# Seven products over the whole contraction for all eight pairs of weight blocks, and one pool for the large scratch

## The chip, the cores and the metric

The kernel runs on one core of a Trainium2 chip. The metric is device time in microseconds (us) of one execution; the time of a kernel is the median of its runs. A run goes through these engines: TensorE (PE, with its weight load PEld), VectorE (DVE), ScalarE (ACT), GpSimd (POOL) and SyncE (SP), which here only issues DMAs. Each engine works through its own queue of instructions in order; semaphores make one engine wait for another.

## The reference, cut to what matters

One layer of a decoder trunk over 528 tokens (16 meta tokens and 512 of the sequence), width 2048: an RMS norm, one input projection, three token mixers side by side (gated DeltaNet with 6 heads, GLA with 5, forgetting attention with 5), a SiLU gate per head, and one output projection with a residual add and a final norm.

```python
h = rms_norm(x, norm_w)
proj = h @ w_in                      # 2048 x some 7600 columns, split into heads
...
o_fox = forgetting_attention(to_heads(fq) * FOX_D ** -0.5, to_heads(fk), to_heads(fv), log_f)
o_fox = o_fox.reshape(fz.shape) * jax.nn.silu(fz)
o = jnp.concatenate([o_dn, o_gla, o_fox], axis=-1)[:, PAD:]
return x + o @ w_out                 # then the final rms_norm
```

Each attention head needs four blocks of 128 columns of `w_in`: `fk`, `fq`, `fv` and `fz` (keys, queries, values, gate). All arithmetic is float32; a product is formed from two parts of each factor (`hi` and `lo`), as hi·hi + hi·lo + lo·hi, so three matmuls stand for one.

## The kernel before, in words

**Layout.** Activations are held transposed: 16 chunks of 128 contraction rows by 528 tokens, each as two tiles, `xh[k]` and `xl[k]`. A block of 128 weight columns is two halves of 128 x 1024 (`w_in[b, 0]` for chunks 0 to 7, `w_in[b, 1]` for chunks 8 to 15). `load_half` (L145) loads one half into `raw`, ACT writes `hi` (L166), DVE writes `lo` (L167). `raw`, `hi` and `lo` have two buffers each (pool `wp`).

**A plain block** (`inproj`, L237) multiplies both halves with all tokens. With the meta tokens it is 96 matmuls of 264 columns, without them 48 of 512 columns (L223).

**Order.** DeltaNet gates; two groups of three DeltaNet heads (`dn_keys`, `dn_values`, `dn_queries`, `dn_inverse`, `dn_mix`); the five GLA gates; three `gla_pair`s; five `fox_head`s; the output projection. The order of the instructions on every engine is written at build time by a list scheduler, which goes by program order as priority, by its own model of times and by which buffers are free; `split` is given priority over everything, and some small matmuls of GLA are tied behind a numbered matmul of a projection (`PLACE`, L191).

**Seven products.** For attention heads 1 to 4 two blocks `one` and `two` form a pair, (`fk`, `fq`) or (`fv`, `fz`). Cut tokens into two halves of 264 (`lo_`, `hi_`), the contraction into two halves (`up`: chunks 0 to 7, `dn`: 8 to 15) and the columns into `one` and `two`: the 2 x 2 by 2 x 2 block product needs eight products, or seven if sums of operands are used (Strassen and Winograd). The sums of activations are `t1`, `t2` and `t4`, made on POOL with their `hi` and `lo` parts on ACT and DVE (`x_sums`, L462), and a difference that overwrites `xh[k][:, HT:]` and `xl[k][:, HT:]` (`x_last`, L489: three DVE operations per chunk ahead, then one on ACT and one on DVE once no plain block needs the old values). The sums of weights, `ti`, are made in DRAM by DMAs of POOL's queue: four copies and four accumulating copies per pair (`in_jobs`, L441). The output projection has such sums of its own (`tw`, `out_jobs`). Both are "chores": every `load_half` issues `rate` steps of them, paced behind a `split`.

Here only four of the eight chunks of each half (`NK = 4`) go by the seven products; the other four (`r0`, `r1`) go by plain ones in the same function `inproj_pair` (L504), which loads its weights with `tile_of` (L512) in six tiles and splits them in pieces of 512 columns. A pair is 180 matmuls: 144 of 264 columns and 36 of 248. The first pair, (`fk`, `fq`) of head 1, is left out (`SKIP = 1`) and runs as two plain blocks (L1108 to L1110), so there are seven pairs. For the first of them the sums are used late (`LATE = 1`).

**Buffers.** `hp`: 32 tiles for `xh` and `xl`. `zp`: 12 tiles of 128 x 528 for the gates, and for `t1`, `t2`, `t4` of chunks 0 to 2. `six`: 8 large buffers (128 x 1584) for the operands of the mixers, the sums of chunk 3, and so on. `row`: 7 of 128 x 531. `t15`: 6 of 128 x 384. Gates of the first eight heads are written to DRAM (`zd`) and read back for the output projection (L1256); the other eight stay in `zp` and in the tiles of the attention heads.

Of the kernel before, what the change touches and what calls it, by code (L numbers as in the profile page):

```python
# [18 lines left out]
P = 128  # L19
D = 2048  # L20
KT = D // P
NM = 16
# [12 lines left out]
NK = 4  # L35
H1 = 1
SKIP = 1
LATE = 1
ZK = 3
# [44 lines left out]
def tile_hybrid_trunk(ctx, tc, xT, xtok, mtok, w_gate, w_in, w_out, w_dn, consts, lmask, fin_w, out, dbg=None):  # L84
# [7 lines left out]
    zp = pool("zp", 12)  # L92
    six = pool("six", 8)
# [34 lines left out]
    wgk = cst.tile([48, 320], F32R, name="wgk")  # L128
# [30 lines left out]
    def split(raw, hi, lo, neg=False):  # L159
        with tc.high_priority(offset=1000000):  # L160
            if neg:
                pace[0] = A.activation(hi, raw, AF.Copy, scale=-1.0).ins  # L162
                pace[1] = V.scalar_tensor_tensor(out=lo, in0=raw, scalar=-1.0, in1=hi.bitcast(F32), op0=ALU.mult,  # L163
                                                 op1=ALU.subtract).ins
            else:
                pace[0] = A.copy(hi, raw).ins  # L166
                pace[1] = V.tensor_tensor(out=lo, in0=raw, in1=hi.bitcast(F32), op=ALU.subtract).ins  # L167
# [9 lines left out]
    def load_rows(src, name):  # L177

        n = src.shape[-1]
        raw = row(f"raw{name}")[:, :n]  # L180
        nc.sync.dma_start(out=raw, in_=src)
        hi, lo = (zp.tile([P, 512], F32R, tag="zs", name=f"w{i}{name}")[:, :n] for i in ("hi", "lo"))
        split(raw, hi, lo)
        return hi, lo
# [171 lines left out]
    zs = {}  # L356

    def gate_z(kind, h, t=None):
        parts = inproj((kind, h), meta=False)
        p_, t0, n = parts[0]  # L360
        z = row(f"z{kind}{h}")[:, :T]
        V.tensor_tensor(out=z[:, :S], in0=p_, in1=rstd[:, t0 : t0 + n], op=ALU.mult)  # L362
        if t is None:
            t = zp.tile([P, T], F32, tag="zs", name=f"zs{kind}{h}")[:, :S]
        silu(t, z[:, :S], f"{kind}{h}")
        zs[kind, h] = t
# [18 lines left out]

    raw = row("rawgk")[:48, :320]
# [5 lines left out]
    glr = cst.tile([48, T], F32R, name="glr")  # L392
# [36 lines left out]
    ti = drp.tile([len(PAIRS), P, 4, KC], F32, name="ti")  # L429
    tw = drp.tile([SH // 2, 4, P, 1024], F32, name="tw")  # L430
    zd = drp.tile([DN_HEADS + GLA_HEADS, P, S], F32, name="zd")
# [9 lines left out]
    def in_jobs(n):  # L441
        h, one, two = PAIRS[n]
        w = lambda key, half: w_in[BLOCK_OF[key, h], half][:, :KC]
        o = [ti[n][:, i] for i in range(4)]
# [16 lines left out]

    def x_sums(ks):  # L462
        for k in ks:
            t = row(f"xd{k}")
# [4 lines left out]
            def parts(n, i, r):  # L469
                o = zp.tile([P, T], F32R, tag="zs", name=f"{n}_{k}") if o3 is None else o3[:, i]  # L470
                A.copy(o[:, :HT], r)
                V.tensor_tensor(out=o[:, HT:], in0=r, in1=o[:, :HT].bitcast(F32), op=ALU.subtract)
# [16 lines left out]
    def x_last(last):  # L489

        f = lambda u: u[:, HT:].bitcast(F32)
        for k in range(NK):
            if not last:
                if k % 2 == 0:
                    t = row(f"xe{k}")
                xr[k] = a = t[:, HT * (k % 2) : HT * (k % 2) + HT]
# [7 lines left out]
    def inproj_pair(n, c1, c2, tmp):  # L504
# [5 lines left out]
        lo_, hi_ = slice(0, HT), slice(HT, T)  # L510

        def tile_of(name, *parts, neg=False):  # L512

            raw = wp.tile([P, 1024], F32, tag="raw", name=f"raw{nm}{name}")
            hi = wp.tile([P, 1024], F32R, tag="hi", name=f"whi{nm}{name}")
            lo = wp.tile([P, 1024], F32R, tag="lo", name=f"wlo{nm}{name}")
            o, cuts = 0, []
            for src in parts:
                w = src.shape[-1] * (src.shape[1] if len(src.shape) == 3 else 1)
                dst = raw[:, o : o + w]  # L520
                nc.sync.dma_start(out=dst.rearrange("p (h c) -> p h c", h=2) if len(src.shape) == 3 else dst, in_=src)
                o += w
            for c in range(0, o, 512):
                cuts.append(slice(c, c + 512))
                split(raw[:, cuts[-1]], hi[:, cuts[-1]], lo[:, cuts[-1]], neg)
            return [(hi[:, c], lo[:, c]) for c in cuts]

        def mm(p_, w, xx, first=False, last=False, cols=slice(0, HT)):

            hi, lo = w  # L530
            todo = [(hi, j, i) for j in range(len(xx)) for i in range(2)] + [(lo, j, 0) for j in range(len(xx))]
            for i, (wt, j, part_) in enumerate(todo):
                m = PE.matmul(p_[:, cols], wt[:, j * P : (j + 1) * P], xx[j][part_][:, cols],  # L533
                              start=first and i == 0, stop=last and i == len(todo) - 1, skip_group_check=True)
# [4 lines left out]
        up = range(NK)  # L539
        dn = range(8, 8 + NK)  # L540
        r0, r1 = range(NK, 8), range(8 + NK, 16)
        both = lambda b_, c: w_in[b_].rearrange("h p c -> p h c")[:, :, c]
        head_, rest_ = slice(0, KC), slice(KC, 1024)
        dead = slice(NM, HT)
        nm = f"{b1}_"
        a, b = bank("a"), bank("b")
        w1, w2 = tile_of("1", both(b1, head_))
        mm(a, w1, xs_(up, lo_), True, True)
        A.copy(ta, a[:, :HT])
        mm(b, w2, xs_(dn, lo_), True)  # L550
        def two():
            nonlocal d
            d = bank("d")
            w1, w2 = tile_of("2", ti[n][:, 0:2], neg=True)
            mm(d, w1, sums("t1"), True, True)
            A.copy(tb, d[:, :HT])
            mm(a, w2, sums("t2"), False, True)
            V.tensor_tensor(out=tb, in0=a[:, :HT], in1=tb, op=ALU.add)

        def three():  # L560
            nonlocal c
            c = bank("c")
            w1, w2 = tile_of("3", both(b1, rest_))
            mm(b, w1, xs_(r0, lo_))
            mm(b, w2, xs_(r1, lo_), False, True)
            V.tensor_tensor(out=c1[:, lo_], in0=b[:, :HT], in1=ta, op=ALU.add)
            mm(c, w1, xs_(r0, hi_), True)
            mm(c, w2, xs_(r1, hi_))

        c = d = None  # L570
        for f in (three, two) if n < LATE else (two, three):
            f()
        w1, w2 = tile_of("4", ti[n][:, 2:4])
        mm(a, w1, xs_(up, hi_), False, True)
        A.copy(ta, a[:, :HT])
        mm(c, w2, xs_(dn, hi_), False, True)
        V.tensor_tensor(out=c1[:, hi_], in0=c[:, :HT], in1=tb, op=ALU.add)  # L577
        w1, w2 = tile_of("5", w_in[b2, 0][:, rest_], w_in[b2, 1][:, head_], neg=True)
        mm(d, w1, xs_(r0, hi_))
        mm(a, w2, sums("t4"), cols=dead)  # L580
        mm(a, w1, xs_(r0, lo_), cols=dead)
        w1, = tile_of("6", w_in[b2, 1][:, rest_], neg=True)
        mm(d, w1, xs_(r1, hi_), False, True)
        V.scalar_tensor_tensor(out=c2[:, hi_], in0=d[:, :HT], scalar=-1.0, in1=ta, op0=ALU.mult, op1=ALU.subtract)
        mm(a, w1, xs_(r1, lo_), False, True, cols=dead)
# [28 lines left out]
    def first_sums():  # L614

        s1 = six.tile([P, SH // 2, 256], F32, tag="six", name="s1")
        for j in pairs:
            a, b = (zs[heads[2 * j + i]] for i in range(2))
            raw[j] = r = dict(a11=a[:, t0], a12=b[:, t0], a21=a[:, t1], a22=b[:, t1], s1=s1[:, j], s3=a[:, t1])
# [76 lines left out]
    def dn_inverse(g, st):  # L696
        an, anm = st["an"], st["anm"]
        ab = six.tile([NN * 4 + H, 1024], F32, tag="six", name=f"ab{g}")
# [819 lines left out]
```

## Time and profile before

| what | value |
|---|---|
| median of 3 runs (range) | 1006.03 us (1005.71 to 1006.59) |
| span of the profiled execution (its own time, first to last instruction) | 1004.3 us |
| instructions | 19785 |
| PE busy | 988.2 us, 98% |
| PEld, DVE, ACT, POOL busy | 90%, 64%, 46%, 25% |
| mean granted TensorE clock | 0.998 |
| moved by DMA | 152.56 MB in 62401 packets |

A row of the timeline or of the chain of waits begins with the start and the length in us; a row of a group of instructions gives line, engine, operation, tiles written and read, shape and count, and then busy time and mean length of one in ns. "Busy" counts overlapping instructions once; a single matmul is shown longer than the distance to the next one, because matmuls overlap. So the cost of a matmul in a dense stream is taken from the length of a stretch divided by the count in it. A row of the windows view gives the busy time of each engine in a stretch, with the number of instructions, the granted clock and the share of time in which the DMA engines moved data.

### The profile page before, as it was taken

Reading aid. Unit: us, or ns where it says so; the run is one execution under the profiler, and the core shown is the slowest. Engines: PE = TensorE matmul, PEld = TensorE weight load, DVE = VectorE, ACT = ScalarE, POOL = GpSimd, SP = SyncE. Lnnn points to the kernel's source line nnn. Section 1 sums busy time; section 2 is a strip of 40 time slices with the busy share of each in tenths; the row PEclk is TensorE's granted clock in tenths of the full one; section 3 lists DMA queues with packets and bytes.
Section 4 is the critical chain, followed back from the end, with each engine's and each line's share of the span. In section 5 each row is a group of like instructions: output and inputs, shape, how many; then the busy total and the mean of one; then the engine's idle time right before and its main releaser. Section 6 shows DMA issues by size and latency. Waiting matters only on the chain.

```text
span 1004.3 us, 19785 instructions
## 1 busy us (share of the span) xinstructions
PE 988.2 (98%) x7866; PEld 905.9 (90%) x7866; DVE 642.0 (64%) x1389; ACT 460.8 (46%) x1041; POOL 249.2 (25%) x280
## 2 busy tenths in 40 slices
PE   9999999999999999999999999999999999999996
PEld 7899999899999888899989988899999998888885
DVE  6365877964666895244565674866464667677673
ACT  6653524344455344144445453554444444444454
POOL 1032433322322345113040720311212123000060
PEclk9999999999999999999999999999999999999999
DMA  9635567665555777956722222243333375457534
GB/s 350 248 124 171 147 146 128 151 187 157 114 113 120 209 268 200 207 110 141 185 65 91 66 74 65 81 130 126 116 117 126 119 244 176 145 168 232 180 112 168
DMA packets 62401, 152.56 MB, mean 152 GB/s; under 512 B 12925, under 2 KB 16173, under 8 KB 62052
## 3 DMA queue, kind: packets, MB, share of 16 engines
q1 hardware_dynamic: 40112, 109.80, 33.0%
q0 software_dynamic: 11136, 31.46, 15.3%
q10 hardware_dynamic: 11060, 10.03, 3.5%
q8 instruction: 62, 1.02, 0.4%
q14 instruction: 31, 0.25, 0.1%
HBM read 143.99 MB, written 38.60 MB: 182 GB/s over the span
## 4 chain that ended last, share of the span: by engine, by line
PE 89%; DVE 5%; DMA 2%; issue 1%; ACT 1%; ACTq 0%; POOL 0%; SPq 0%; DVEq 0%; POOLq 0%
PE pp L223 41%; PE pp_a L533 6%; PE pa L1295 5%; PE pq L1295 4%; PE pp L277 4%; PE pt L1295 4%; PE pp_d L533 3%; PE pp_c L533 3%; PE pp_b L533 3%; PE ps L1295 2%; DVE wlo L167 1%; PE pss L983 1%; PE pr L1295 1%; DVE ot L717 1%; PE pgate L377 1%
## 5 line engine op out<-in xcount | busy, mean ns | idle before, releaser
L223 PE MATMUL pp<-xl,whi 128*128 128x264 f32 (+2 forms) x1120 | 284.6, 306 | 0.0
L223 PE MATMUL pp<-xh,whi 128*128 128x264 f32 (+2 forms) x1120 | 282.7, 305 | 0.8 <-DVE fqk L341 0.8
L223 PE MATMUL pp<-xh,wlo 128*128 128x264 f32 (+2 forms) x1120 | 282.2, 305 | 0.5 <-DVE wlo L167 0.5
L223 PEld LDWEIGHTS pp<-xh,whi 128*128 128x128 f32 x1120 | 186.4, 188 | 10.4 <-DVE fqk L341 1.0
L223 PEld LDWEIGHTS pp<-xh,wlo 128*128 128x128 f32 x1120 | 186.6, 189 | 9.6 <-DVE wlo L167 1.0
L223 PEld LDWEIGHTS pp<-xl,whi 128*128 128x128 f32 x1120 | 187.1, 189 | 8.9 <-issue 0.2
L167 DVE TENSOR_TENSOR wlo<-raw,whi 128x1024 fp32r<-128x1024 f32 (+1 forms) x124 | 129.9, 1058 | 86.2 <-ACT whi L166 76.7
L166 ACT CAST whi<-raw 128x1024 fp32r<-128x1024 f32 (+1 forms) x124 | 109.9, 902 | 158.4 <-PE pp L223 107.3
L350 POOL TENSOR_SCALAR stc<-cv 128x528 f32<-128x528 f32 (+1 forms) x18 | 28.1, 1561 | 118.0 <-DVE cv L598 96.7
L598 DVE SCALAR_TENSOR_TENSOR cv<-pb,cpk,cv 128x528 f32<-128x528 f32 (+1 forms) x54 | 41.1, 761 | 0.7
L1319 POOL TENSOR_TENSOR acc<-acc,fw 128x512 f32<-128x512 f32 x4 | 6.3, 1598 | 126.8 <-ACT sqf L1316 126.8
L162 ACT ACTIVATE whi<-raw 128x512 fp32r<-128x512 f32 x35 | 20.5, 624 | 25.0 <-PE pp_c L533 10.2
L166 ACT CAST whis<-raws 128x1024 fp32r<-128x1024 f32 x16 | 16.4, 1049 | 27.5 <-DMA raws<-tw 14.0
L163 DVE SCALAR_TENSOR_TENSOR wlo<-raw,whi 128x512 fp32r<-128x512 f32 x35 | 23.0, 685 | 8.8 <-ACT whi L162 8.7
L1295 PE MATMUL pa<-wloo,oh 128*128 128x512 f32 x72 | 28.4, 395 | 0.0
L1295 PE MATMUL pa<-whio,ol 128*128 128x512 f32 x72 | 28.4, 395 | 0.0
L533 PE MATMUL pp_a<-xh,whi 128*128 128x264 f32 (+1 forms) x112 | 27.9, 283 | 0.0
L533 PE MATMUL pp_a<-xl,whi 128*128 128x264 f32 (+1 forms) x112 | 27.7, 281 | 0.0
L167 DVE TENSOR_TENSOR wlos<-raws,whis 128x1024 fp32r<-128x1024 f32 x16 | 19.3, 1221 | 11.9 <-ACT whis L166 11.9
L350 POOL TENSOR_SCALAR stdz<-zdz 128x512 f32<-128x512 f32 x6 | 11.3, 1882 | 61.9 <-DVE zdz L362 61.9
L1295 PE MATMUL pa<-whio,oh 128*128 128x512 f32 x72 | 25.9, 400 | 0.0
L1121 POOL TENSOR_TENSOR vf<-vf,rstd 128x528 f32<-128x528 f32 x4 | 6.4, 1606 | 77.2 <-DVE vf L577 77.2
(499 smaller groups left out, 2262.2 us busy)
## 6 DMA issues: line engine op xcount, KB each, us to landing
raw<-in_w_in SPq DMA_DIRECT2D x96, 512.0 KB, 3.9
tw<-in_w_dn POOLq DMA_DIRECT2D x24, 512.0 KB, 5.6
ti<-in_w_in POOLq DMA_DIRECT2D x42, 256.0 KB, 5.4
raw<-ti SPq DMA_DIRECT2D x14, 512.0 KB, 4.1
rawo<-in_w_out SPq DMA_DIRECT2D x13, 512.0 KB, 3.4
raws<-tw SPq DMA_DIRECT2D x12, 512.0 KB, 4.3
raw<-in_w_in SPq DMA_DIRECT2D x21, 256.0 KB, 3.1
xt<-in_xtok SPq DMA_DIRECT2D x8, 512.0 KB, 8.6
```

Of the source, the lines that this page charges most:

```text
L162: pace[0] = A.activation(hi, raw, AF.Copy, scale=-1.0).ins
L163: pace[1] = V.scalar_tensor_tensor(out=lo, in0=raw, scalar=-1.0, in1=hi.bitcast(F32), op0=ALU.mult, op1=ALU.subtract).ins
L166: pace[0] = A.copy(hi, raw).ins
L167: pace[1] = V.tensor_tensor(out=lo, in0=raw, in1=hi.bitcast(F32), op=ALU.subtract).ins
L223: mm = PE.matmul(p_[:, :nt], wt[:, j * m : (j + 1) * m], xx[k][:, t0 : t0 + nt], start=(k == 0 and wt is hi and xx is xh), stop=(k == KT - ...
L277: mm = PE.matmul(ps[:, :S], wt[:, j * P : (j + 1) * P], xx[k][:, NM:T], start=(k == 0 and wt is hi and xx is xh), stop=(k == KT - 1 and wt ...
L350: G.tensor_scalar_max(t, src, LOW)
L377: PE.matmul(pgate[a][:, :HT], wg[k // 8][:, k % 8, :], xx[k][:, a * HT : (a + 1) * HT], start=(k == 0 and xx is xh), stop=(k == KT - 1 and ...
L533: m = PE.matmul(p_[:, cols], wt[:, j * P : (j + 1) * P], xx[j][part_][:, cols], start=first and i == 0, stop=last and i == len(todo) - 1, ...
L598: V.scalar_tensor_tensor(out=c, in0=pb[:, t0 + w : w + T], scalar=cwc[:, blk, w : w + 1], in1=c, op0=ALU.mult, op1=ALU.add)
L717: V.tensor_tensor(out=t3, in0=a3[:, j + 1 :, j : j + 1].to_broadcast([NN * 4 + H, m, j]), in1=a3[:, j : j + 1, 0:j].to_broadcast([NN * 4 + ...
L1295: PE.matmul(p_, o_[:, s], w_, start=(first and n == 0), stop=(last and n == 2), skip_group_check=True)
```

## The change

`NK` becomes 8, `SKIP` 0; `LATE` and `ZK` go. Each of now eight pairs is seven `product`s of 24 matmuls (hi parts of 8 chunks twice, then lo parts), six of 264 columns and one of 248: 168 matmuls. Each product loads one half with `load_half`, so that chores are stepped in the pairs too. The sums `t1`, `t2`, `t4` are now negated and the weights are not. `x_sums` and `x_last` run over 8 chunks; `x_sums` is moved into `gla_pair` and `fox_head(0)`, queued on POOL behind a named instruction (`anchor`); `x_last(True)` runs ahead of the first pair. The weight sums are whole contiguous halves, and the rate of the chores falls from 2 to 1 at the second DeltaNet group.

Pool `zp` goes and `six` has 14 buffers: gates three to a buffer, a buffer of sums per chunk, `gcn` for two constants of GLA, scratch of GLA (`ds`) and of the inverse (`ot`), four buffers for gates read back, and all accumulators. Small tiles (`xm`, `um`, `a32`, `gkm`, `gst`) move to `t15`. The gates of GLA heads 2 to 4 and of attention heads 0 to 3 are now also written to DRAM and, except for the last of the plain heads, read back into a `row`.

```diff
-NK = 4
+NK = 8
-SKIP = 1
-LATE = 1
-ZK = 3
+SKIP = 0
...
-    zp = pool("zp", 12)
-    six = pool("six", 8)
+    six = pool("six", 14)
...
-    ti = drp.tile([len(PAIRS), P, 4, KC], F32, name="ti")
+    ti = drp.tile([len(PAIRS), 4, P, KC], F32, name="ti")
...
     def x_sums(ks):
         for k in ks:
+            with tc.issue_after(anchor[-1]):
+                x_sum(k)
...
+    def x_sum(k):
             t = row(f"xd{k}")
-            o3 = six.tile([P, 3, T], F32R, tag="six", name=f"t_{k}") if k >= ZK else None
+            o3 = six.tile([P, 3, T], F32R, tag="six", name=f"t_{k}")
...
+        def product(p_, src, xx, first=False, cols=slice(0, HT)):
+            hi, lo = load_half(src, f"{b1}_{len(order)}")
+            todo = [(hi, j, i) for j in range(NK) for i in range(2)] + [(lo, j, 0) for j in range(NK)]
             for i, (wt, j, part_) in enumerate(todo):
                 m = PE.matmul(p_[:, cols], wt[:, j * P : (j + 1) * P], xx[j][part_][:, cols],
...
+        product(a, w_in[b1, 0], xs_(up, lo_), True)
         A.copy(ta, a[:, :HT])
+        product(b, w_in[b1, 1], xs_(dn, lo_), True)
+        V.tensor_tensor(out=c1[:, lo_], in0=b[:, :HT], in1=ta, op=ALU.add)
+        product(a, ti[n, 1], sums("t2"))
+        A.copy(tb, a[:, :HT])
+        d = bank("d")
+        product(d, ti[n, 0], sums("t1"), True)
+        V.tensor_tensor(out=tb, in0=d[:, :HT], in1=tb, op=ALU.add)
+        product(a, ti[n, 2], xs_(up, hi_))
         A.copy(ta, a[:, :HT])
+        c = bank("c")
+        product(c, ti[n, 3], xs_(dn, hi_), True)
+        V.scalar_tensor_tensor(out=c2[:, hi_], in0=d[:, :HT], scalar=-1.0, in1=ta, op0=ALU.mult, op1=ALU.subtract)
         V.tensor_tensor(out=c1[:, hi_], in0=c[:, :HT], in1=tb, op=ALU.add)
+        product(a, w_in[b2, 1], sums("t4"), cols=dead)
         A.activation(c2[:, dead], a[:, dead], AF.Copy, scale=-1.0)
...
-            d = wk.tile([P, S], F32, tag="gd", name=f"gdd{p}{li}")[:R]
+            d = ds[li % 3][:R]
...
-        G.tensor_tensor(out=d4, in0=d4, in1=k4, op=ALU.mult)
+        anchor.append(G.tensor_tensor(out=d4, in0=d4, in1=k4, op=ALU.mult).ins)
+        x_sums(XSUM.get(p, ()))
...
-            G.tensor_copy(v4, v[:, 0:NM].unsqueeze(1).to_broadcast([P, 2 * NB, NM]))
+            anchor.append(G.tensor_copy(v4, v[:, 0:NM].unsqueeze(1).to_broadcast([P, 2 * NB, NM])).ins)
...
             vhi, vlo, v3, vm = values(v)
+            x_sums(XSUM.get(9, ()))
             evac(inproj(("fq", h), meta=False), qT, scale=float(P) ** -0.5)
...
+                if h == H1:
+                    x_last(True)
                 inproj_pair(n, kT, qT, qk[:, 1])
...
+        if h < FOX_HEADS - 1:
+            nc.sync.dma_start(out=zd[DN_HEADS + GLA_HEADS + h], in_=z)
...
-    AHEAD = {(0,-1):(2,(-1,-2,-3,-4),(-5,-6,-7),(0,1,2,3))}
-    XSUM = {1: (0,), 2: (1,2), 9:(3,)}
+    AHEAD = {(0, -1): (2, (-1, -2, -3, -4, -5, -6, -7, -8), (0, 1, 2, 3)), (1, -1): (1,)}
+    XSUM = {0: (0,), 1: (1, 2), 2: (3,), 9: (4, 5, 6, 7)}
...
+        if i < NP - 1:
+            z = row(f"zp{i}")[:, :S]
+            nc.sync.dma_start(out=z, in_=zd[SH + i])
```

More of the change, by code (lines that the diff above doesn't have):

```diff
@@ L1253, in tile_hybrid_trunk @@
         next(chores[0], None) or chores.pop(0)
-    for i in [*range(SH, SH), *range(SH)]:
-        key = ("dz", i) if i < DN_HEADS else ("gz", i - DN_HEADS)
-        zs[key] = zp.tile([P, T], F32, tag="zs", name=f"zr{i}")[:, :S]
-        nc.sync.dma_start(out=zs[key], in_=zd[i])
+    zr = [six.tile([P, 3, S], F32, tag="six", name=f"zr{j}") for j in pairs]
+    for i in range(SH):
+        zs[heads[i]] = zr[i // 2][:, i % 2]
+        nc.sync.dma_start(out=zs[heads[i]], in_=zd[i])
     plain = heads[SH:]
```

168 lines of the change are left out of this document (54 added, 114 removed).

## The prediction

> **What bounds the kernel now.** I read the page first, then its chain of waits.
>
> ```profile
> PE 988.2 (98%) x7866; PEld 905.9 (90%) x7866; DVE 642.0 (64%) x1389; ACT 460.8 (46%) x1041; POOL 249.2 (25%) x280
> PE   9999999999999999999999999999999999999996
> PE 89%; DVE 5%; DMA 2%; issue 1%; ACT 1%; ACTq 0%; POOL 0%; SPq 0%; DVEq 0%; POOLq 0%
> ```
>
> TensorE has work in every slice but the last, and 89% of the chain is PE. So a matmul taken away is worth its distance to the next one, as long as nothing else comes late. What can come late is a split weight half, a sum of activations, or an operand of attention. The windows view cuts the stretch that the change touches.
>
> ```profile
> core 0: us, PE busy (x) PEld busy (x) DVE busy (x) ACT busy (x) POOL busy (x), PEclk, DMA share, GB/s
> 390.00:500.00 110.00, 108.89 (x955) 101.72 (x955) 45.20 (x99) 43.18 (x120) 25.90 (x26) 1.00 0.71 163
> 500.00:614.00 114.00, 111.08 (x1555) 100.50 (x1554) 76.76 (x160) 55.80 (x149) 38.32 (x32) 1.00 0.24 75
> 614.00:643.50 29.50, 29.50 (x283) 26.10 (x282) 16.89 (x30) 13.38 (x38) 7.26 (x8) 1.00 0.18 55
> 643.50:823.60 180.10, 177.97 (x1437) 175.10 (x1436) 112.58 (x296) 85.07 (x197) 29.50 (x29) 1.00 0.41 132
> ```
>
> PE idles 1.1 us before 500, 2.9 us to 614 (GLA and head 0), nothing under the two plain blocks of head 1, and 2.1 us in 180 us of pairs. The granted clock is full throughout. The largest stalls of the pairs and of GLA stand in the view of waits (us, times, longest):
>
> ```profile
> PE pss L983 <- issue: 1.9, 1, 1.9
> PE pp_b L533 <- DVE wlo L167: 1.1, 1, 1.1
> PE pp_a L533 <- ACT fqk L575: 1.0, 1, 1.0
> ```
>
> **Matmuls removed and added.** Their prices come from the chain in order of time (start, length, count) and from four rows of PE's timeline.
>
> ```profile
> 76.43 21.64 PE pp L223 x177
> 823.59 11.10 PE pa L1295 x48
> ```
>
> ```profile
> 691.07 1.07 PE L533 MATMUL pp_a<-t,whi 128*128 128x248 f32 x8
> ...
> 693.37 0.63 PE L533 MATMUL pp_a<-xh,wlo 128*128 128x248 f32 x4
> 693.83 0.38 PE L1170 MATMUL pfx<-ident,fp 128*128 128x128 f32 x2
> ```
>
> A matmul of 264 columns costs 21.64/177 = 0.122 us, one of 512 columns 11.10/48 = 0.231. The 24 of 248 columns from 691.07 up to 693.83 cost 2.76/24 = 0.115.
> (a) Each of the seven pairs there now loses 12 matmuls of 248 columns (180 to 168): 7 x 12 x 0.115 = 9.7 us.
> (b) The two plain blocks, 96 x 0.122 + 48 x 0.231 = 22.8 us, become a pair, 144 x 0.122 + 24 x 0.115 = 20.4: 2.5 us, with rounding.
> Together -12.2 us, all on the chain. Nothing else takes PE work away.
>
> **Weights for the pairs.** A product of 24 matmuls needs one 512 KB half in 24 x 0.122 = 2.94 us, seven halves a pair where 5.5 served. The two `raw` buffers bound the supply: a buffer waits for the landing, for the copy to `hi` and for the subtraction to `lo`, and is loaded again. Of the two rows of landings, the first is of 644 to 824 and the second of 390 to 500, where chores load the DMA engines.
>
> ```profile
> L166 ACT CAST whi<-raw 128x1024 fp32r<-128x1024 f32 x82 | 85.9, 1048 | 132.9 <-PE pp L223 106.9 <-DMA scr<-an 10.4 <-DMA raw<-in_w_in 8.0
> L167 DVE TENSOR_TENSOR wlo<-raw,whi 128x1024 fp32r<-128x1024 f32 x82 | 102.4, 1249 | 66.2 <-ACT whi L166 56.7 <-PE ps L814 4.3 <-PE pp L223 3.6
> DMA to landing us min/median/max: 2.6/3.7/4.5
> DMA to landing us min/median/max: 3.2/4.8/8.0
> 643.50:823.60 180.10, 159.09 (x1260) 154.12 (x1259) 1.00 0.41 132
> ```
>
> A cycle is 3.7 + 1.05 + 1.25 = 6.0 us for two products, 3.0 per product; with 4.8 it is 7.1, or 3.55. Demand is slower than 2.94, since attention's small matmuls lie between: the last row is the pairs' own PE time, so 180.1 - 159.1 - 2.1 = 19 us over 7 pairs, 0.39 us a product, hence one half per 3.33 us. At 3.0 nothing is lost; at 3.55 it is 0.2 us a product. The chores now fall to rate 1 and reach into the pairs: of 144 steps, 100 are issued by the end of head 0 and the last 44 with the first 44 of 56 products. Ends: 0 and 0.2 x 44 = 9 us. The DMA share in the pairs was 0.41, nearer to the quiet window for everything but those chores, and their 28 transfers are spread over 150 us. I take +1.5, with the extra dumps of gates on SP in it (each waits there for its gate, and the next half's load is queued behind it).
>
> By the fit of the Trainium skill (DMA: Bandwidth & Descriptors, "Anatomy of one DMA — SWDGE (gpsimd) path": about 2.0 us plus bytes over 436 GB/s) a half would land in an estimated 3.2 us, the cycle would be 5.5, and 2.75 a product would hide even under 2.94. The rows' 3.7 do not agree, and they decide.
>
> **Sums of activations, and the cover that goes.** These are the first operands at risk. On POOL a chunk is seven operations; ACT and DVE make three pairs of parts of it.
>
> ```profile
> L475 POOL TENSOR_TENSOR xd<-xh,xd x8: 744/854/1754, 523.3 to 644.5; 128x264 f32<-128x264 f32 x8
> L475 POOL TENSOR_TENSOR xd<-xd,xl x8: 746/790/932, 524.1 to 646.6; 128x264 f32<-128x264 f32 x8
> L475 POOL TENSOR_TENSOR xd<-xh x4: 883/1470/5195, 504.2 to 636.3; 128x264 f32<-128x264 f32 x4
> L472 DVE TENSOR_TENSOR t<-xd,t x12: 420/428/1055, 523.6 to 650.3; 128x264 fp32r<-128x264 f32 x12
> L497 DVE TENSOR_TENSOR xe<-xh,xh x4: 423/706/996, 635.7 to 637.3; 128x264 f32<-128x264 f32 x4
> ```
>
> Four more chunks are 28 x 0.85 = 24 us of POOL, 12 x 0.43 = 5 us of DVE for parts and 12 x 0.5 = 6 us for `x_last`, and 12 ACT copies. Before, the last sums were made up to 650.3, under the two plain blocks (614.0 to 643.5) and beside the first pair, whose order was turned round for them. Now chunks 4 to 7 start behind the copy of `v4` in head 0, and the pair follows `fq` of head 0 at once, its third product needing `t2` of all eight.
>
> ```profile
> 622.22 1.27 POOL L1021 TENSOR_TENSOR gqd<-gqd,gqk 64x512 f32<-64x512 f32 x1 [21.77 <-ACT gqd L1020]
> 623.44 0.28 POOL L1092 COPY v<-vf 128x128 f32<-128x128 f32 x1
> 613.86 0.28 PE L223 MATMUL pp<-xh,whi 128*128 128x264 f32 x1
> 631.00 0.40 PE L223 MATMUL pp<-xh,whi 128*128 128x512 f32 x1
> ```
>
> That copy ran at 623.44, because POOL works in order and stood behind GLA's `gqd`. If it stays there, the last `t2` is ready at 623.7 + 24 - 2 = 646, while PE, starting the pair at 613.9, gets to its third product after 2 x 2.94 us and 5.4 us of small matmuls of GLA and head 0 (the 96 matmuls of `fk` took from 613.86 to 631.00, 17.1 us, where 96 x 0.122 is 11.7), at 625: a wait of 21 us, less what other matmuls fill. If GLA's last pair lets POOL go 12 us earlier, more than half of it goes. Ends 0 and +20; I take +2. Why low: DVE has 37 us free in 500 to 614 and POOL 76, and GLA now gets `kq`, `ds` and its rows from 14 large buffers where 8 had to be shared:
>
> ```profile
> 461.24 0.94 PE L855 MATMUL psn<-y,kd 128*128 128x128 f32 x6 [0.57 <-ACT y L851]
> 463.05 0.76 DVE L341 TENSOR_TENSOR gqk<-pp,rstd 128x264 f32<-128x264 f32 x2
> ```
>
> `gqk` of the first GLA pair was written 0.9 us after DeltaNet's last `psn` had released its buffer. That wait goes, and GLA may start ahead of it. On PE, busy 108.9 of 110 us there, it is worth nothing by itself.
>
> **GLA and head 0 with more on DVE and POOL.** Three chunks instead of two or three are queued there behind `dd`, and the gates' dumps come to SP. Ends: -2 (the stalls of 1.9 and 1.0 us go) and +4 (DVE at 67% of 500 to 614 delays some small matmul); +1.
>
> **Edits at nothing.** POOL issues 64 rather than 56 transfers for `ti`:
>
> ```profile
> ti<-in_w_in POOLq DMA_DIRECT2D x42, 256.0 KB, 5.4
> zr<-zd SPq DMA_DIRECT2D x8, 256.0 KB, 5.4
> ```
>
> They are hidden under 200 us and more of projections before use. The seven gates read back for the output projection are issued with the plain splits; PE has other heads' matmuls meanwhile, and without that cover one landing, 5.4 us, would show. Scratch moved to `six` and `t15`, the evacuations (eight per pair as before) and the negated sums (one operation for one) cost nothing as long as the order stays.
>
> **Sum.** -12.2 + 1.5 + 2 + 1 = -7.7. The profiled execution has a span of 1004.3 us, which becomes 996.6; the median of the runs is 1006.0, so 1.7 us lie outside the span or between runs, and I forecast 1006.0 - 7.7 = 998.3. About 0.2% (2 us) is what a measurement of this kernel can tell from no change.
>
> **Rivals.** *First pair waits for its sums* (the slower side). The place is the third product of (`fk`, `fq`) of head 1, the price up to 21 us, of which attention of head 0 fills perhaps 5: 15.5 rather than 2, so 998.3 + 13.5 = 1012. It decides (no gain left) when `t2` of the last chunk is ready after about 635. For it: POOL's order, the cover of 29.5 us that goes, sums that were late even with half the chunks. Against it: freed buffers, and a scheduler that can place head 0's other work first.
>
> By the rule of the Trainium skill (SBUF — State Buffer, "The single rule") an operation of DVE with two inputs in SBUF and one of POOL that reads SBUF shut each other out for a whole instruction. This trace agrees as far as it goes: L497 takes 423 to 996 ns for one shape. With 28 x 0.57 = 16 us more on POOL the wait would be an estimated 37 us.
>
> *Weights bind the pairs.* If every half takes the 3.55 us of the busy window, 0.2 us a product over all 56 is 11 us in place of the 1.5: 998.3 + 9.7 = 1008. It decides when the mean of a half passes 3.5 us. For it: 3.0 is already above 2.94, and where attention's matmuls lie apart from the products nothing stretches the demand. Against it: `wlo` stalled PE only 1.1 us in seven pairs, though their loads were fewer.
>
> *The gain is whole*: nothing comes late, 1006.0 - 12.2 = 994; the range's lower bound lets GLA's stalls go as well, 992.
>
> **Chances.** Forecast, whole gain included (993 to 1003): 0.52. First pair waits (1003 to 1022): 0.30; for 1 in 10 of it the wait is short enough to come out the same. Weights bind (1000 to 1014): 0.18, a third of it faster or the same. Faster 0.52 + 0.03 = 0.55, same 0.03 + 0.03 = 0.06, slower 0.27 + 0.12 = 0.39. The range of 8 in 10 is 992 to 1016; the forecast's own is 993 to 1003.
>
> **What would show it.** Right: 168 matmuls a pair, eight pairs of about 24 us, PE idle under 5 us in them, no wait on `t` of more than 2 us. Wrong, by the first rival: a row at L533's successor with a wait for `t` on DVE or `xd` on POOL of 10 us or more near 620; by the second: waits of `pp` for `wlo` or `whi` of 0.2 us and more in most products, with landings near 5 us. The forecast falls too if the matmuls' spacing in the pairs is over 0.122, or if the stretch 390 to 614 grows by more than 5 us.

## The result, and the profile after

The changed kernel takes 1121.4 us (median of 5 runs, 1120.1 to 1128.3), the kernel before 1005.7 (now of five runs as well): 1.116 times as long (95% interval 1.113 to 1.119). The forecast was 998.3 us, in a range of 992 to 1016.

The profiled execution is the longest of the five (1128.3 us); its span of 1126.6 us is 122.3 more than before. From its page, the busy times, PE's and the clock's slices, and the chain by engine:

```profile
PE 1011.0 (90%) x7806; PEld 922.6 (82%) x7806; DVE 670.7 (60%) x1394; ACT 479.0 (43%) x1036; POOL 278.8 (25%) x317
PE   8998999989999999985969594978988976999997
PEclk9999999989999999996999797999989996999999
PE 60%; DMA 12%; DVE 10%; ACT 4%; issue 2%; POOL 1%; ACTq 0%; SPq 0%; DVEq 0%; POOLq 0%
```

PE is idle for 1126.6 - 1011.0 = 115.6 us, where it was 16.1; and although it has less to do, it is busy 22.8 us longer. The saving is there: the matmuls stream 1,993,421 columns where they streamed 2,020,205, and at 0.122 us per 264 that is 12.4 us (forecast 12.2). It is lost in five places. The windows view by stage (DeltaNet and the first projections; GLA and head 0; the first pair; the other seven; head 4 alone; the output projection):

```profile
core 0: us, PE busy (x) PEld busy (x) DVE busy (x) ACT busy (x) POOL busy (x), PEclk, DMA share, GB/s
0.00:505.00 505.00, 491.35 (x3742) 456.06 (x3742) 307.66 (x685) 220.77 (x498) 124.19 (x158) 0.99 0.58 169
505.00:674.00 169.00, 134.25 (x1753) 121.68 (x1754) 93.72 (x191) 68.44 (x184) 60.57 (x62) 0.86 0.32 97
674.00:735.00 61.00, 39.69 (x273) 37.73 (x271) 44.50 (x92) 22.87 (x48) 23.80 (x33) 0.83 0.47 166
735.00:919.00 184.00, 165.54 (x1260) 160.84 (x1261) 102.77 (x222) 82.58 (x152) 42.43 (x41) 0.96 0.67 189
919.00:951.00 32.00, 13.02 (x46) 9.83 (x45) 13.47 (x46) 10.38 (x28) 9.92 (x12) 0.59 0.82 280
951.00:1126.60 175.60, 167.19 (x739) 136.49 (x737) 108.64 (x158) 73.95 (x128) 17.88 (x12) 0.99 0.43 151
```

PE's idle time by stage is 14, 35, 21, 18, 19 and 8 us. In the four rows in the middle no engine is busy throughout: PE is at 41 to 90%, DVE at most at 73%. And where PE waits, the granted clock falls, to 0.59 in the fifth row.

To compare kernels whose stages overlap differently I use PE's work as the clock: the columns that the matmul rows of a trace have streamed up to a moment. The *lag* at an amount of work is the time at which a run reaches it minus the time at which the kernel before does (its times: 900,000 columns at 447 us, 1,200,000 at 605, 1,350,000 at 682, 1,600,000 at 803, 1,900,000 at 942). The changed kernel has 12.4 us less to do in all, so what it loses in time is its last lag less 12.4.

| run | DeltaNet (to 900k) | GLA, head 0 (to 1200k) | first pairs (to 1350k) | later pairs (to 1600k) | output projection (to 1900k) | time, us |
|---|---|---|---|---|---|---|
| changed kernel | 11 | 55 | 85 | 108 | 134 | 1128.3 (median 1121.4) |
| e1_early_slots | 6 | 17 | 61 | 87 | 112 | 1106.3 |
| e2_no_weight_sums | 3 | 46 | 64 | 66 | 92 | 1086.1 |
| e3_rate2 | 13 | 57 | 75 | 78 | 102 | 1096.7 |
| e4_no_reload | 12 | 56 | 86 | 110 | 120 | 1114.7 |
| f1_slots_rate2 | 13 | 26 | 54 | 57 | 82 | 1076.4 |
| f2_skip1 | 17 | 25 | 61 | 63 | 89 | 1086.1 |
| f3_no_act_sums | 11 | 18 | 32 | 35 | 60 | 1054.8 |
| f4_skip1_no_reload | 13 | 20 | 57 | 59 | 69 | 1066.3 |
| g1_zp_six | 18 | 31 | 60 | 63 | 76 | 1070.5 |
| g3_noact_noreload | 14 | 19 | 33 | 35 | 44 | 1038.1 |
| g4_all_out | 8 | 10 | 23 | 26 | 36 | 1030.0 |
| h1_sums_spread | 15 | 46 | 63 | 65 | 81 | 1076.1 |
| i1_skip1_select | 14 | 21 | 57 | 58 | 71 | 1068.1 |

The experiments are single runs, each beside the kernel before on the same chip (1005.4 to 1008.4 us). The changed kernel's own five runs spread over 8 us, so from times alone I read no difference below that; where it lies is read from the lags. f2, f4 and i1 stream 5952 columns more, the two plain blocks, so their last levels compare to 3 us only.

The columns are cut at fixed amounts of work, not where pairs end: 1350k lies in the third pair, 1600k in the eighth. Cut instead where the first pair begins (1226k), where the second begins (1272k) and where the last ends (1615k), the lag of the changed kernel grows by 22 us in the first pair and by 28 in the seven others. DeltaNet's lag differs by 5 us between runs whose edits lie behind it (the changed kernel and e1, f1 and g1), so I read no smaller difference of lags.

### The profile page after: what moved, and what is told of

The parts are those of the page before. It is cut to its first block, busy times and chain, and to the rows that moved or that the text cites. A ratio compares the mean times of both kernels' runs of the same rounds, so it can differ in the third digit from the quotient of the medians.

```text
span 1126.6 us, 19730 instructions
## 1 busy us (share of the span) xinstructions
PE 1011.0 (90%) x7806; PEld 922.6 (82%) x7806; DVE 670.7 (60%) x1394; ACT 479.0 (43%) x1036; POOL 278.8 (25%) x317
## 4 chain that ended last, share of the span: by engine, by line
PE 60%; DMA 12%; DVE 10%; ACT 4%; issue 2%; POOL 1%; ACTq 0%; SPq 0%; DVEq 0%; POOLq 0%
PE pp L215 30%; DMA raw<-ti 5%; PE pa L1261 4%; PE pq L1261 4%; PE pp_a L530 3%; PE pt L1261 3%; DMA raw<-in_w_in 3%; DVE wlo L158 3%; ACT whi L157 2%; PE ps L1261 2%; DMA sc<-ab 1%; PE pp_c L530 1%; PE pp_d L530 1%; PE pr L1261 1%; DMA iv<-sc 1%
## 5 line engine op out<-in xcount | busy, mean ns | idle before, releaser
L215 PE MATMUL pp<-xl,whi 128*128 128x264 f32 (+2 forms) x1072 | 264.9, 307 | 0.0
L158 DVE TENSOR_TENSOR wlo<-raw,whi 128x1024 fp32r<-128x1024 f32 x134 | 171.2, 1278 | 144.7 <-ACT whi L157 128.8
L157 ACT CAST whi<-raw 128x1024 fp32r<-128x1024 f32 x134 | 140.4, 1048 | 262.8 <-PE pp L215 130.3
L1285 POOL TENSOR_TENSOR accs<-accs,fw 128x512 f32<-128x512 f32 x12 | 17.9, 1521 | 152.9 <-ACT sqf L1282 152.9
L530 PE MATMUL pp_a<-t,whi 128*128 128x264 f32 (+1 forms) x256 | 35.3, 291 | 12.6 <-ACT fqk L539 12.3
L530 PEld LDWEIGHTS pp_a<-t,whi 128*128 128x128 f32 x256 | 33.4, 197 | 13.3 <-ACT fqk L539 12.6
L530 PE MATMUL pp_d<-t,whi 128*128 128x264 f32 x128 | 21.3, 328 | 18.0 <-ACT whi L157 18.0
L530 PEld LDWEIGHTS pp_d<-t,whi 128*128 128x128 f32 x128 | 19.4, 225 | 19.5 <-ACT whi L157 19.5
L530 PE MATMUL pp_a<-xh,whi 128*128 128x264 f32 x128 | 33.5, 293 | 0.9 <-ACT whi L157 0.9
L530 PE MATMUL pp_a<-xl,whi 128*128 128x264 f32 x128 | 33.1, 291 | 0.1
```

The source lines that it names most:

```text
L215: mm = PE.matmul(p_[:, :nt], wt[:, j * m : (j + 1) * m], xx[k][:, t0 : t0 + nt], start=(k == 0 and wt is hi and xx is xh), stop=(k == KT - ...
L1285: G.tensor_tensor(out=acc[tb, cc], in0=acc[tb, cc], in1=fw[cc], op=ALU.mult)
```

## The experiments

### GLA and head 0: the order in which large buffers are handed out

In the changed kernel PE has no projection to fill GLA's waits with. From its view of waits, 505 to 674 us, and its timeline of DVE:

```profile
PE pss L950 <- DVE kq L936: 19.1, 5, 8.8
PE pss L950 <- ACT gdm L981: 7.7, 1, 7.7
PE pp L215 <- DVE gqk L333: 2.9, 1, 2.9
```

```profile
513.73 0.42 DVE L928 TENSOR_TENSOR kq<-gqk 128x256 f32<-128x256 f32 x1
524.51 0.76 DVE L333 TENSOR_TENSOR gqk<-pp,rstd 128x264 f32<-128x264 f32 x2
```

The evacuation of the next pair's projection (L333) stands at 524.5, behind the chain of scores that begins at 513.7. The last matmul of that pair's keys and queries was at 499; until 524.5 they held three of the four PSUM banks (two halves of 264 columns and one of 512), so the next projection could not start. Yet by the addresses of the built program the buffer that `gqk1` takes is that of `kT1`, whose last readers are six matmuls of DeltaNet, done at 498.5. So it had been free for 26 us:

```profile
497.71 0.83 PE L809 MATMUL pks<-sn,kT 128*128 128x128 f32 x6
```

What stands ahead of it in the program are other buffers of the same pool: `kq2`, the scratch `ds`, first written in GLA itself, and `t_0`, the sums of chunk 0.

```diff
+    G.memset(kq[2][:, 0:1], 0.0)
+    for k in range(4):
+        o3_[k] = six.tile([P, 3, T], F32R, tag="six", name=f"t_{k}")
+        G.memset(o3_[k][:, 0, 0:1].bitcast(F32), 0.0)
...
-            o3 = six.tile([P, 3, T], F32R, tag="six", name=f"t_{k}")
+            o3 = o3_.get(k) or six.tile([P, 3, T], F32R, tag="six", name=f"t_{k}")
```

> The changed kernel with one edit: five of its large buffers (the scratch kq2 and the sums of chunks 0 to 3) get a tiny first write ahead of the first GLA pair, so that they are handed out before gqk1 and gqk2; all work stays. Theory S (buffers): large buffers are handed out in the order of their first writes, so the evacuation of the next GLA projection (gqk1 at 524.5 us, gqk2 at 590.5, fqk0 at 644.5) stands behind the scratch and the sums of the pair before, while four PSUM banks are full and PE has no projection to fill with; the lag of PE's work grows by 20, 10 and 16 us at these three places. S expects the evacuations about 20 us earlier against the chain of scores, PE idle under 10 us in GLA and about 1121 - 40 = 1080 us. Theory L (load): the sums' extra work on POOL and DVE slows the chain of scores itself; the order of evacuations changes nothing; 1115 to 1125 us.

It took 1106.3 us. From its timeline of DVE:

```profile
493.08 0.76 DVE L333 TENSOR_TENSOR gqk<-pp,rstd 128x264 f32<-128x264 f32 x2
502.50 0.42 DVE L928 TENSOR_TENSOR kq<-gqk 128x256 f32<-128x256 f32 x1
```

The evacuation now comes ahead of the scores, and the lag grows by 11 us in GLA where it grew by 44: theory S holds for the place, with 33 of the 40 us that it named, though no work was taken away. (The lag at GLA's end is 17 for 55; 5 of that difference lie in DeltaNet.) But the time fell by only 15 us against the median, 22 against the profiled run. The lag then grows by 30 us in the first pair, where it grew by 22, and by 36 in the other seven, where it grew by 28: half of the gain is given back to waits that come next. So 33 us of lag came from nothing but an order that the scheduler fixes when the kernel is built.

The other side of the same mechanism is the last run of this group. It starts from g1_zp_six (below) and moves sums forward, away from the first pair:

```diff
-    XSUM = {0: (0,), 1: (1, 2), 2: (3,), 9: (4, 5, 6, 7)}
+    XSUM = {0: (0, 1), 1: (2, 3), 2: (4,), 9: (5, 6, 7)}
```

> The kernel with gates in large buffers (run before in this call), and the sums spread over the GLA pairs: chunks 0 and 1, 2 and 3, and 4 behind the three pairs, 5 to 7 behind head 0 (before 0; 1 and 2; 3; 4 to 7). POOL has six microseconds less to do before the first pair: if its start is set by POOL's chain, 5 to 8 us are gained (about 1053 us from 1060). Against it: the buffer of chunk 4 is asked for ahead of fqk0 again, whose evacuation moves behind GLA's scores, by the mechanism of theory S: no gain or up to 10 us lost.

It took 1076.1 us, where g1 took 1070.5. GLA loses 15 us more (lag 46 for 31), with `t_4` ahead of `fqk0` again (evacuated at 635.4 us, in g1 at 618.7), and the first pair, with a chunk less to wait for, loses 12 us less (17 for 29). A sum is paid for in either place.

### The pairs: sums of weights, and when the chores run

From the changed kernel, 674 to 919 us: two waits of PE; the landings of `raw`; three pieces of the chain; two rows of POOL's queue.

```profile
PE pp_d L530 <- ACT whi L157: 18.0, 7, 5.0
PE pp_a L530 <- ACT fqk L539: 12.3, 1, 12.3
```

```profile
DMA to landing us min/median/max: 3.0/4.2/11.4
```

```profile
724.40 11.43 DMA raw<-ti
761.53 8.19 DMA raw<-ti
788.10 8.96 DMA raw<-ti
```

```profile
717.78 1.31 POOL L1084 TENSOR_TENSOR fqk<-fqk,rstd 128x528 f32<-128x528 f32 x1 [14.81 <-DVE fqk L552]
...
720.67 2.96 POOL L437 DMA_DIRECT2D tw<-in_w_dn  x6
```

A half that lands in 11.4 us is one that was asked for just after POOL had issued six transfers of 512 KB within 3 us, after it had stood 14.8 us at an operation that needs the first pair's result. The other two halves follow four and five such transfers, at 758 to 762 and 783 to 788 us. Two runs take this apart: one without the sums of weights, one with the chores early.

```diff
-        product(a, ti[n, 1], sums("t2"))
+        product(a, w_in[b1, 1], sums("t2"))
...
-                jobs(*[in_jobs(-k - 1) if k < 0 else out_jobs(k) for k in n])
+                jobs(*[out_jobs(k) for k in n if k >= 0])
```

> The changed kernel without the weight sums: no copies into ti, the four products that read ti read halves of w_in instead (results scaled by 0.1 so that they stay in range; heads 1 to 4 are not the reference's). Theory W (weights): 64 transfers of 512 KB on POOL's queue and late chores slow the landings; without them the DeltaNet part gets back its lag of about 12 us and the pairs their waits for whi (24 us), about 1121 - 35 = 1086 us. If the landings are only slow because loads are issued late (each behind its buffer), the sums of weights cost little: 1110 us or more.

```diff
-    AHEAD = {(0, -1): (2, (-1, ..., -8), (0, 1, 2, 3)), (1, -1): (1,)}
+    AHEAD = {(0, -1): (2, (-1, ..., -8), (0, 1, 2, 3))}
```

> The changed kernel with the chores at rate 2 throughout, as before the change, so that none of them is left for the pairs. Theory W expects the waits of PE for whi in the pairs to fall from 24 us to under 8 and more lag ahead of 500 us (up to 10 us more): 1100 to 1112 us. If the chores in the pairs do not matter: 1118 to 1130 us, all of the difference in the DeltaNet part.

They took 1086.1 and 1096.7 us. In both the lag of the seven later pairs grows by 1 us where it grew by 28, and that of the first pair by 18 where it grew by 22. From e3, 676 to 888 us:

```profile
PE pp_d L530 <- ACT whi L157: 0.8, 3, 0.3
```

```profile
DMA to landing us min/median/max: 3.1/3.3/6.2
```

With all sums of weights still made and read, the halves land in 3.3 us and PE waits 0.8 us. So it is not the number of loads nor the reading of `ti` that held the pairs, but the 25 transfers of `tw` that the lower rate left for them: 28 us there, and in the first pair some 5, no more than runs differ by. That it is their bunches, more than their number, is read from the three halves above; no run spread them. e2 gains 10 us more, in DeltaNet (lag 3 against 13 at rate 2).

Both edits of GLA and pairs together:

> The changed kernel with both edits: the five buffers handed out early and the chores at rate 2. The two losses lie at different places (GLA: 500 to 660 us; the pairs), alone they gave back about 17 and 25 us. If the causes are separate: about 1121 - 42 = 1079 us, with the first pair's wait for its sums of activations (14 us) and the tail as they were. If one hides the other: 1090 us or more.

1076.4 us: the two gains add (15 + 25 = 40 against the median; measured 45).

### The first pair: what its cover was worth

In f1 the first pair still costs 28 us of lag, by waits of 9.9 and 5.1 us in it. It was made plain again, with `x_last(True)` behind it (and without the eight transfers of this pair's sums):

```diff
-SKIP = 0
+SKIP = 1
...
-                if h == H1:
-                    x_last(True)
                 inproj_pair(n, kT, qT, qk[:, 1])
...
+            if h == H1:
+                x_last(True)
             v = row(f"vf{h}")[:, :T]
```

> The kernel with early buffers and rate 2, and the first pair (fk, fq of head 1) as two plain blocks again: seven pairs by the seven products. Theory F (the first pair waits for its sums, 14 us in one wait and more while DVE and POOL make sums and differences): the blocks cost 9 us of PE more (29.5 measured before, against 20.4 for a pair) and give back the 25 to 30 us by which the stretch of GLA's end and the first pair lags: 1055 to 1065 us. If the first pair only inherits a lag made earlier: 1079 + 2.5 = 1081 us or more.

1086.1 us, ten more: up to 1350k the lag grows by 36 us for 28, and the 5952 columns are 2.7 us. The blocks covered nothing, and the wait moved with them. POOL's timeline shows one reason, and the rows of PE and ACT the wait:

```profile
664.18 1.43 POOL L487 TENSOR_TENSOR xd<-xd,xl 128x264 f32<-128x264 f32 x2
683.19 0.63 POOL L1102 TENSOR_SCALAR_AFFINE_SELECT fc<-fc 128x512 f32<-128x512 f32 x1 [17.58 <-DMA fc<-gd]
683.80 2.59 POOL L487 TENSOR_TENSOR xd<-xd,xl 128x264 f32<-128x264 f32 x2
```

```profile
698.15 3.89 PE L530 MATMUL pp_a<-t,whi 128*128 128x264 f32 x16 [15.16 <-ACT fqk L539]
```

```profile
692.96 0.42 ACT L479 ACTIVATE t<-xd 128x264 fp32r<-128x264 f32 x1 [0.47 <-POOL xd L487]
...
697.74 0.36 ACT L539 COPY fqk<-pp_a 128x264 f32<-128x264 f32 x1
```

What PE waited for last is not a sum. It is ACT's copy of the pair's first product (L539) out of the bank `pp_a`, which the product of `t2` writes next. In ACT's queue this copy stands behind the last part of a sum (692.96) and behind the gate and softmax of head 0 and a copy of `x_last`, so the last 4 us of the wait are theirs. In the changed kernel it is the same: last part at 699.4, copy at 704.5.

In the middle of the sums POOL stands 17.6 us at a select of head 0, until a load lands that ACT issued late. The select was ordered behind the last sum (on top of f2, and with the read back of g1):

```diff
-        G.affine_select(out=cm, ...)
+        with tc.issue_after(last_[0]):
+            G.affine_select(out=cm, ...)
```

> The kernel with early buffers, rate 2, gates read back into large buffers, two plain blocks in place of the first pair, and POOL's select on fc of head 0 ordered behind the last sum of activations. In the run with the plain blocks alone POOL stood 17.6 us at that select in the middle of the sums, waiting for the load fc<-gd that ACT issued at 680, and the next pair waited 15.2 us. Theory P (POOL's order): the sums of chunks 4 to 7 end some 16 us earlier, under the plain blocks, the wait of 15 us falls below 5 us, and the lag of 61 us after the first pairs falls to about 40: about 1055 to 1062 us (1086 - 6 for the gates in large buffers - 20). If the cover is worthless because something else holds the pair (ACT's copies, the differences of x_last on DVE): a wait of over 8 us remains, 1068 us or more.

1068.1 us, and PE still waits 12.6 us; up to 1350k the lag grows by 36 us, as in f2. Theory P falls. POOL now stands 12.9 us between two sums, at 663 to 676, and what it waits for is the parts of the first sums (rows of PE, POOL and ACT):

```profile
694.35 0.45 PE L1140 MATMUL pfx<-ident,fp 128*128 128x128 f32 x1 [12.64 <-ACT fqk L540]
```

```profile
676.34 1.53 POOL L488 TENSOR_TENSOR xd<-xh,xd 128x264 f32<-128x264 f32 x2 [12.93 <-DVE t L480]
```

```profile
672.49 1.05 ACT L157 CAST whi<-raw 128x1024 fp32r<-128x1024 f32 x1 [5.95 <-PE pp L215]
675.14 0.27 ACT L1065 CAST fvm<-pwf 128x128 fp32r<-128x128 f32 x1 [1.61 <-PE pwf L1063]
675.31 0.74 ACT L479 ACTIVATE t<-xd 128x264 fp32r<-128x264 f32 x2
```

ACT's copies of the parts (L479) stand in its queue behind the split of a weight half, and that split waits for PE to leave the buffer. So the sums go forward only as PE goes through the blocks that are to cover them. And the sums hold up those blocks. A little earlier POOL ran sums without a gap until 663.4; beside them DVE's split of a weight half took 9.78 us, and PE waited for it:

```profile
654.72 9.78 DVE L158 TENSOR_TENSOR wlo<-raw,whi 128x1024 fp32r<-128x1024 f32 x1 [5.57 <-ACT whi L157]
```

```profile
664.55 0.80 PE L215 MATMUL pp<-xh,wlo 128*128 128x512 f32 x1 [7.07 <-DVE wlo L158]
```

A split takes 1.25 us otherwise (last section). In f2 it was 8.39 us, and a wait of 5.7. All this is read from the rows; I made no run that frees the copies from ACT's queue, or the split from POOL's sums, so neither is shown to be the whole cause.

What the sums of activations cost in all was measured by leaving them out of f1 (products read parts of `xh` and `xl`):

> The kernel with early buffers and rate 2, but without the sums of activations (t1, t2 and t4 are replaced by parts of xh and xl, results scaled by 0.1; heads 1 to 4 are not the reference's): 56 operations of POOL, 24 each of ACT and DVE and eight large buffers are gone. Theory F plus buffers: no wait in the first pair, free buffers for the tail, so about 1079 - 30 - 10 = 1040 us. If the sums are not the cause of what is left: over 1070 us.

1054.8 us, 22 less, of which 13 lie in the first pair (its part of the lag is 15 for 28) and 7 in GLA. The expected 10 us of the tail did not come (25 as in f1). The 15 us that remain lie beside head 0's attention, which nothing covers now: PE waits 7.0 us at one of its transposes (by the profile for the same copy of ACT), and 6.9 in g4 below, where the lag grows by 13 us there. The rest of them is not separated.

### The output projection: gates read back

```diff
-            z = row(f"zp{i}")[:, :S]
-            nc.sync.dma_start(out=z, in_=zd[SH + i])
+            z = rstd[:, :S]
```

> The changed kernel without the seven reads of gates back from DRAM at the output projection: their parts are made from rstd, which is resident (output not the reference's). Theory T (tail): the output projection started 19 us after the last pair, at 951 us, since the reads went out at 940.6, behind the loads of the accumulators; without them it starts beside head 4's attention and the time falls by 15 to 21 us, to 1100 to 1106 us. If the large buffers of the accumulators, or the row buffers, hold it: 1116 to 1122 us.

1114.7 us. The output projection starts 0.1 us after the last pair (at 920.9), where it started 32 us after; but only 7 us come off the median, 14 off the profiled run. From SP's and PE's timelines of the changed kernel:

```profile
920.79 3.92 SPq L1225 DMA_DIRECT2D zr<-zd  x8
940.58 2.93 SPq L1235 DMA_DIRECT2D zp<-zd  x3
```

```profile
950.88 0.63 PE L1261 MATMUL pa<-whio,oh 128*128 128x512 f32 x1
951.31 0.63 PE L1261 MATMUL pa<-wloo,oh 128*128 128x512 f32 x1
...
952.52 0.40 PE L1261 MATMUL pa<-wloo,oh 128*128 128x512 f32 x1
952.75 0.39 PE L1261 MATMUL pa<-whio,oh 128*128 128x512 f32 x1
```

The reads `zp` wait for row buffers that head 4 holds and for the loads of the accumulators. A real remedy reads them into three large buffers, which come free when the last pair has used the sums (on top of f1):

```diff
+    zpb = [six.tile([P, 3, S], F32, tag="six", name=f"zpb{j}") for j in range(3)]
+    for i in range(len(heads) - SH - 1):
+        nc.sync.dma_start(out=zpb[i // 3][:, i % 3], in_=zd[SH + i])
...
+            z = zpb[i // 3][:, i % 3]
```

> The kernel with early buffers and rate 2, and the seven gates read back into three large buffers, asked for ahead of the others, in place of small row buffers. Theory T: the reads go out at the end of the last pair (some 867 us), when eight buffers of sums come free, and not 20 us later behind head 4's row buffers; the output projection starts within 10 us of the pairs' end in place of 32, and the time falls by 12 to 20 us from 1076 to about 1060 us. If the row buffers are not what held it: 1072 us or more.

1070.5 us, 6 less than f1. The reads go out at 875.2 us, 2 us behind the pairs, where f1's go out 22 us behind; the output projection starts 12.6 us after the pairs, not 32 (its part of the lag falls from 25 to 13). Expected were 10 us and 12 to 20 off the time: the place is right, and DeltaNet's lag, which the edit does not touch, was 5 us larger in this run.

With the reads left out, and two plain blocks, or no sums:

> As the run with early buffers, rate 2 and two plain blocks, and without the reads of seven gates back from DRAM (parts made from rstd; output not the reference's). If the four causes (order of buffers, chores in the pairs, sums of the first pair, reload at the output projection) make up the loss, this comes within 25 us of the kernel before: 1035 to 1050 us by the 7 to 16 us that the reload cost alone; the rest would then be the DeltaNet part and the tail's other waits.

> The kernel with early buffers and rate 2, without sums of activations and without the reads back (output not the reference's). The tail lost 27 us of PE time in all kernels with the reads and 11 us without. If the other 11 us come from buffers that the sums hold to the end of the pairs, they go here too: 1055 - 27 = 1028 us. If not: 1055 - 16 = 1039 us.

1066.3 (against 1086.1 with the reads) and 1038.1 us (against 1054.8): the reads cost 17 to 20 us once PE is not held elsewhere. f4 was expected below 1050 and is not: the first pair is still in it. In g3 some 8 us of the tail stay; freeing the sums' buffers does not give them back. PE waits 3 to 5 us at a time in head 4's transposes in these runs; why the output projection does not fill them stays open.

### Nothing but the products

> As the last, and without the weight sums too (loads from w_in): only the matmuls, loads and splits of eight pairs of seven products are left of the change, and the new pools. If the supply of weights (one half of 512 KB per product) holds the pairs, they lag here too, by 0.2 us a product or 11 us: 1020 us or more. If the products by themselves run as forecast: at or below the kernel before, 995 to 1012 us, by what is left of the lag in DeltaNet and head 0.

1030.0 us, between the two cases. From its waits of PE, 740 us to the end:

```profile
PE pp_d L531 <- ACT whi L157: 0.6, 2, 0.3
```

The seven later pairs run as forecast: the lag grows by 1 us over them, with 0.6 us of waits for a half. What is left over the kernel before is mostly 8 us in DeltaNet, 13 at head 0 and 10 at head 4.

## Why the prediction was wrong

**Matmuls: right.** 168 a pair, 12.4 us less work for the 12.2 of terms (a) and (b). In g4, where nothing else is in the way, the seven later pairs keep pace.

**"Weights for the pairs", +1.5 of a range of 0 to 9: the mechanism was named, the size wrong.** The cycle of 6.0 us holds in a quiet window (landing 3.3 in e3, so even shorter). With chores I took 4.8 us for a landing from 390 to 500 us and spread the 28 transfers evenly over 150 us. POOL issued six at once, and a landing took up to 11.4. Measured: 33 us of lag, 28 of them in the seven later pairs, and 25 us off the median (e3). The range that the rows gave was too narrow on the side of the bunch. The fit of the Trainium skill (DMA: Bandwidth & Descriptors, "Anatomy of one DMA — SWDGE (gpsimd) path") is given for DMAs that GpSimd issues, and these halves are issued by SP; its estimated 3.2 us is still close to e3's 3.3.

**"Sums of activations", +2 between 0 and 20, and the rival on them: the place was right, the price was the rival's, the reasons were not.** The product of `t2` waited 12.3 us in one piece, and the sums cost 13 us in the first pair and 7 in GLA (f3). But the wait ended with ACT's copy behind the sums, not with `t` or `xd`, as the rival said. And "the cover of 29.5 us that goes" was not the cause: put back (f2), it covered nothing. What I left out is that the sums work on other queues than POOL's: ACT's copies stand behind them, and DVE's splits beside them (9.78 us for 1.25 in i1).

**GLA with "its rows from 14 large buffers where 8 had to be shared": the step that failed most.** I counted buffers, and not the order in which they are handed out. The lag grows by 44 us in GLA; e1 takes 33 of them back at that place with five tiny writes. Forecast: +1, with ends -2 and +4. The sign that I named, "the stretch 390 to 614 grows by more than 5 us", is the one that fired first.

**"Edits at nothing": the reads back were not hidden.** "PE has other heads' matmuls meanwhile" fails, because the last head has nothing after it but the output projection, which waits for these reads. I priced the loss of the cover at one landing, 5.4 us. It is 17 to 20 us once PE is not held elsewhere: the reads start 22 us behind the pairs (940.6 against 918.6), and head 4's attention then runs alone.

**DeltaNet:** no term in my sum; measured 11 us of lag. Without sums of weights it is 3 and 8, with them 6 to 18. The rest is not separated.

**Idle PE was priced at its length.** Each of the sums above counts waits alone. PE's busy time is 22.8 us longer, with 12.4 us less work, so 35 us of the 122 are matmuls that took longer, 32 of them at a lower clock (last section).

The two named rivals, added, would have given 1012 + 10 = 1022. All forecasts of the slower side took one mechanism each; four came together.

## What to carry to other kernels

Where a scheduler fixes the order of queues when the kernel is built, a pool of more buffers can be slower: look in the trace for a first write into a buffer whose last use lies well before, and take such buffers early. Count background transfers at the moment when they are issued: a queue that was blocked lets them go in a bunch. And in a kernel whose PE is 98% busy, test the removal of a wait together with the ones behind it: alone, e1 gave 15 to 22 of its 33 us and e4 7 to 14 of its 17 to 20.

## What the runs showed of the hardware

**The granted clock falls with the waits.** Before, it was 0.998 over the whole span; in the changed kernel it is 0.95, and 0.59 from 919 to 951 us, where PE waits 19 of 32 us. The rows of the output projection above show the price: the first two matmuls of 512 columns are 0.43 us apart (950.88, 951.31), and those from 952.52 on 0.23. The Trainium skill (TensorE: Matmul & The Clock Gate, "Part 1: The HAM clock gate") says that PE runs at half its clock after an idle window of about 3.4 us until it has been busy for as long; the trace agrees in the ratio (0.43 to 0.23), and waits of 4.6 and 5.3 us lie ahead. In the trace's record of the clock, which stands at either 1.0 or 0.5, the lower value holds for 122 us of the changed kernel. PE is busy for 63 us of them and streams 68,016 columns, which at 0.122 us per 264 would take 31. So 32 us of PE's busy time come from the clock.

**One DVE instruction stood through six of POOL.** A split of a half takes DVE 1.25 us; beside POOL's sums it took 5.33, and it ended 1.1 us after they did, about its own length. From the changed kernel's timelines of DVE and POOL:

```profile
675.17 5.33 DVE L158 TENSOR_TENSOR wlo<-raw,whi 128x1024 fp32r<-128x1024 f32 x1 [6.45 <-ACT whi L157]
```

```profile
675.12 2.88 POOL L487 TENSOR_TENSOR xd<-xh,xd 128x264 f32<-128x264 f32 x4
677.97 1.45 POOL L487 TENSOR_TENSOR xd<-xd,xl 128x264 f32<-128x264 f32 x2
```

That is the rule that the prediction cites from the Trainium skill (SBUF — State Buffer, "The single rule"), and more than I drew from it: not one instruction of the other engine, but all that follow one another without a gap. In i1, where POOL's run was longer, the split took 9.78 us and again ended 1.1 us after it. In the changed kernel the next load of `raw` went out as the split ended, at 680.5.
